# A two-group encoder block: the down products by Strassen's algorithm, right operands summed a phase earlier

## The chip, the cores and the metric

The kernel runs on one core of a Trainium2 chip. The metric is the time of one execution on the device, in microseconds (us). Before the change three runs gave a median of 2451.57 us (2447.15 to 2452.31).

## The reference

One layer is applied to two sequences with shared weights: 256 and 1024 tokens, each with 16 meta tokens in front. All is float32, the width is 1024, FF is 2816.

```
h = h + 0.5 * SwiGLU_1(RMSNorm(h))          # (silu(x Wg) * (x Wu)) Wd
u = RMSNorm(h) @ W_in                        # q, k, v of 4 heads; 512 channels for a pooling mixer
h = h + concat(diff_attention(q, k, v), pool(u)) @ W_out
h = h + 0.5 * SwiGLU_2(RMSNorm(h))
out = RMSNorm(h), meta tokens dropped
```

## The kernel before, in words

The 1296 tokens (1280 after the mixer, which drops one set of meta tokens; both sequences share the other) lie along the free axis, channels on the partitions: h is 8 chunks of 128 channels. Every float32 product is three matmuls (`mm3`, lines 161 to 163): both operands are split into a high and a low part, and high x high, low x high and high x low are added in one PSUM bank. The high part is a cast, on ScalarE (`hi_act`, line 146) or GpSimd (`hi_pool`, line 149); the low part is a subtraction, on VectorE (`lo_dve`, line 152) or GpSimd (`lo_pool`, line 155).

The gate and up products go by Strassen's algorithm (Winograd's form): tokens lie in four blocks of 324 (320), two blocks make a half, and the left operand is a pair of FF chunks. `s_parts` makes seven left operands out of the weights of a pair, four of them sums; seven right operands (`T_NAMES`: b11, t1, t2, b22, t3, b21, t4) lie split in SBUF for each half. `seven` runs the seven products in this order, adding in PSUM into three accumulators, A (b11, t2, t3, t4), C (t1, b22) and B (b21). ScalarE keeps three partial sums, VectorE adds the others, ScalarE takes silu of the gate, VectorE multiplies it with the up product (line 488), and SP stores the hidden tiles to device memory (line 490), four per pair of chunks and half. At the head of a feed-forward the first half runs alone for three pairs (`SINGLE1`, `SINGLE2`) while the right operands of the second half are made (`t_loaded`); then both halves run for eight pairs; then the second half runs alone for the first three.

The down product doesn't use the algorithm: for each pair of FF chunks `prep` loads hidden tiles of three blocks (272, 512 and 512 tokens; 256, 512, 512 in the second feed-forward) and splits them; for each of 8 output chunks and each block six matmuls fill a bank, and VectorE adds half of it to h (line 530). For the last pair it goes block by block, so that sums of squares and the norm of a finished block go on beside the next (`norm_tasks`, deferred through a list of small tasks that `pump` takes from between matmuls). The mixer's projections use the same three blocks: three projections first (`lead`), then the others; the value product takes tokens as left operands, in tiles of 128, 96 or 80 rows. At the kernel's end `finish` transposes h by token tiles, normalises and stores; the last block is two tiles.

All DMAs are issued on SP. Weights come through a ring of three raw buffers (`wraw`, 512 KB each) and five pairs of split ones (`wh`, `wl`). The order on each engine is set when the kernel is built: of the instructions whose inputs are expected to be ready, the one that stands first in the program. On the chip each engine then takes its queue in that order.

## Time and profile before

| | |
|---|---|
| median of three runs | 2451.57 us |
| the profiled execution | 2450.31 us, its span 2448.5 us |
| TensorE busy | 2336.4 us, 95% of the span |
| VectorE, ScalarE, GpSimd busy | 62%, 33%, 16% |
| TensorE's mean granted clock | 0.979 of full speed |
| DMA | 264.7 MB, 108 GB/s over the span |

Times are in microseconds from the span's start. PE is TensorE's matmuls, PEld its weight loads, DVE VectorE, ACT ScalarE, POOL GpSimd, SP the engine that issues DMAs. The first down stage runs from 612 to 933, the second from 2118 to 2437; the first gate and up phase from 54 to 612. Matmuls are pipelined, so the length shown for one is more than the distance to the next.

### The profile page before, as it was taken

The numbers are of one execution on the slowest core, as the hardware profiler recorded it, in microseconds if no ns is written. First come the engines' busy times: TensorE is split into PE (matmuls) and PEld (weight loads), VectorE is DVE, ScalarE is ACT, GpSimd is POOL, SyncE is SP. The second block draws the span as 40 slices with busy tenths as digits, with TensorE's granted clock in tenths as the row PEclk, the third lists the DMA queues.
The fourth block names the chain that finished last, engine by engine and source line by source line (L and its number), as shares of the span: only waits on it lengthen the run. The fifth ranks groups of instructions, "written<-read, shape, count | busy, mean of one in ns | idle before, by whom it ended". The sixth has DMA issues, their size and how long they took to land.

```text
span 2448.5 us, 38316 instructions
## 1 busy us (share of the span) xinstructions
PE 2336.4 (95%) x14578; PEld 2181.6 (89%) x14578; DVE 1506.1 (62%) x2834; ACT 803.8 (33%) x1705; POOL 387.6 (16%) x479
## 2 busy tenths in 40 slices
PE   5999999999999998999888898899999999999998
PEld 5899999999888887889778898889999999988886
DVE  7964545448676667344477747685455446667665
ACT  6533333335011123111377723453333334211113
POOL 0000000000111124111376743100000000021112
PEclk7999999999999999999999998999999999999999
DMA  8422222245232224545754154432122216323222
GB/s 234 118 80 72 65 64 75 70 150 174 77 96 79 82 71 134 167 145 159 186 134 124 49 166 154 133 96 74 57 80 73 74 57 222 116 82 96 86 69 86
DMA packets 294591, 264.67 MB, mean 108 GB/s; under 512 B 22048, under 2 KB 254072, under 8 KB 293896
## 3 DMA queue, kind: packets, MB, share of 16 engines
q1 hardware_dynamic: 294408, 262.24, 35.3%
q8 instruction: 114, 1.87, 0.3%
q14 instruction: 69, 0.57, 0.1%
HBM read 190.79 MB, written 75.61 MB: 109 GB/s over the span
## 4 chain that ended last, share of the span: by engine, by line
PE 82%; DVE 8%; DMA 4%; POOL 2%; issue 2%; ACT 1%; SPq 1%; POOLq 0%; ACTq 0%; DVEq 0%
PE bank L162 26%; PE bank L161 26%; PE bank L163 26%; DVE wl L152 1%; DMA v<-v_d 1%; PE bank L893 1%; PE pair L845 1%; PE pair L846 1%; PE bank L242 1%; DMA wraw<-in_ffn_w_up 1%; DMA wraw<-in_ffn_w_gate 1%; DMA cat<-cat_d 1%; POOL l L876 0%; POOL ry L223 0%; DVE h L328 0%
## 5 line engine op out<-in xcount | busy, mean ns | idle before, releaser
L152 DVE TENSOR_TENSOR wl<-wraw,wh 128x512 fp32r<-128x512 f32 x320 | 235.3, 740 | 296.1 <-ACT wh L146 219.8
L530 DVE SCALAR_TENSOR_TENSOR h<-bank,h 128x272 f32<-128x272 f32 (+2 forms) x528 | 313.1, 601 | 155.3 <-PE bank L163 151.3
L161 PE MATMUL bank<-hl,wh 128*128 128x512 f32 (+2 forms) x1056 | 380.4, 360 | 0.0
L162 PE MATMUL bank<-hl,wl 128*128 128x512 f32 (+2 forms) x1056 | 379.4, 359 | 0.0
L163 PE MATMUL bank<-hl,wh 128*128 128x512 f32 (+2 forms) x1056 | 379.1, 359 | 0.0
L146 ACT CAST hl<-hraw 128x272 fp32r<-128x272 f32 (+2 forms) x132 | 72.7, 552 | 517.2 <-PE bank L162 438.6
L155 POOL TENSOR_TENSOR hl<-hraw,hl 128x272 fp32r<-128x272 f32 (+1 forms) x44 | 34.7, 790 | 1239.9 <-ACT hl L146 1148.9
L163 PEld LDWEIGHTS bank<-hl,wh 128*128 128x128 f32 x1056 | 199.2, 189 | 31.6
L161 PEld LDWEIGHTS bank<-hl,wh 128*128 128x128 f32 x1056 | 199.2, 189 | 31.5
L162 PEld LDWEIGHTS bank<-hl,wl 128*128 128x128 f32 x1056 | 199.1, 189 | 31.4
L146 ACT CAST wh<-ws 128x512 fp32r<-128x512 f32 x224 | 138.4, 620 | 252.4 <-PE bank L163 156.0
L451 ACT COPY hid<-bank 128x324 f32<-128x324 f32 (+1 forms) x264 | 112.7, 427 | 279.5 <-PE bank L163 278.9
L152 DVE TENSOR_TENSOR wl<-ws,wh 128x512 fp32r<-128x512 f32 x224 | 153.7, 689 | 73.2 <-ACT wh L146 72.4
L149 POOL TENSOR_SCALAR wh<-wraw 128x512 fp32r<-128x512 f32 x152 | 115.1, 759 | 526.4 <-PE bank L163 245.2
L161 PE MATMUL bank<-t1h,wh 128*128 128x324 f32 (+1 forms) x352 | 110.3, 314 | 9.5 <-ACT wh L146 9.4
L162 PE MATMUL bank<-t1h,wl 128*128 128x324 f32 (+1 forms) x352 | 111.3, 316 | 4.0 <-DVE wl L152 3.9
L161 PE MATMUL bank<-t2h,wh 128*128 128x324 f32 (+1 forms) x352 | 110.2, 313 | 5.1 <-ACT hid L451 5.1
L162 PE MATMUL bank<-t4h,wl 128*128 128x324 f32 (+1 forms) x352 | 109.8, 312 | 3.1 <-DVE wl L152 3.0
L161 PE MATMUL bank<-t4h,wh 128*128 128x324 f32 (+1 forms) x352 | 109.4, 311 | 3.5 <-DVE hid L465 3.5
L161 PE MATMUL bank<-t3h,wh 128*128 128x324 f32 (+1 forms) x352 | 109.4, 311 | 1.8 <-ACT wh L146 1.8
L162 PE MATMUL bank<-t3h,wl 128*128 128x324 f32 (+1 forms) x352 | 109.7, 312 | 1.0 <-DVE wl L152 1.0
L161 PE MATMUL bank<-b21h,wh 128*128 128x324 f32 (+1 forms) x352 | 110.4, 314 | 0.3
(238 smaller groups left out, 6376.1 us busy)
## 6 DMA issues: line engine op xcount, KB each, us to landing
wraw<-in_ffn_w_gate SPq DMA_DIRECT2D x56, 512.0 KB
wraw<-in_ffn_w_up SPq DMA_DIRECT2D x56, 512.0 KB
hraw<-hid_d SPq DMA_DIRECT2D x88, 256.0 KB
wraw<-in_ffn_w_down SPq DMA_DIRECT2D x44, 512.0 KB
hid_d<-hid SPq DMA_DIRECT2D x88, 162.0 KB
hid_d<-hid SPq DMA_DIRECT2D x88, 160.0 KB
k<-k_d SPq DMA_DIRECT2D x32, 260.0 KB
h<-h_d SPq DMA_DIRECT2D x16, 512.0 KB
```

What stands on the lines that cost most here:

```text
L146: nc.scalar.copy(out=out, in_=in_)
L149: nc.gpsimd.tensor_scalar(out=out, in0=in_, scalar1=1.0, scalar2=1.0, op0=ALU.mult, op1=ALU.mult)
L152: nc.vector.tensor_sub(out, in_, hi.bitcast(F32))
L155: nc.gpsimd.tensor_sub(out, in_, hi.bitcast(F32))
L161: nc.tensor.matmul(out=ps, lhsT=wh, rhs=xh, start=first, stop=False, skip_group_check=on)
L162: nc.tensor.matmul(out=ps, lhsT=wl, rhs=xh, start=False, stop=False, skip_group_check=on)
L163: nc.tensor.matmul(out=ps, lhsT=wh, rhs=xl, start=False, stop=last, skip_group_check=on)
L242: nc.tensor.matmul(out=ps[:, j * m : (j + 1) * m], lhsT=r[:, j : j + 1].broadcast_to([m, P]), rhs=ident[:m, :m], start=True, stop=True,)
L451: nc.scalar.copy(out=to[s], in_=ps[s])
L530: nc.vector.scalar_tensor_tensor(out=h[b][:, m], in0=ps, scalar=0.5, in1=h[b][:, m], op0=ALU.mult, op1=ALU.add)
L845: nc.tensor.matmul(out=ps[:, m], lhsT=qs, rhs=kh[:, ks], start=True, stop=False)
L846: nc.tensor.matmul(out=ps[:, m], lhsT=qs, rhs=kl[:, ks], start=False, stop=True)
```

## The change

The hidden values no longer leave the gate and up phase as four tiles per pair and half but as the seven right operands of the down product: `up` forms t3, t1, t2 and t4 on VectorE by four subtractions and stores seven tiles. The down product runs by the same `seven`: the left operands are made by `s_parts` out of four quarters of the down weights (a pair of FF chunks by a pair of output chunks), and the inner sum runs over the pairs of a slice, `nk` of them. A slice is two pairs, the first one is one pair, so there are six slices for 11 pairs. Every product's PSUM sum is added to a quarter of h straight away (`ADDS`), 14 adds for each group of two output chunks (`mp`) and two halves, with no kept partial sums. Right operands lie in two pools of slots, x (ten) and y (32 in the first feed-forward, 26 in the second); those of the next slice are loaded through four staging tiles and split on ScalarE and VectorE while the present slice runs: `early` of them one after each product of the first groups, the rest in the last group, as slots come free. The last group of the last slice runs the halves one after the other, keeping the seven left operands. GpSimd makes no high parts in the down stage any more.

The halves of the first feed-forward are now blocks 0, 1 and 2, 3. The mixer uses the four blocks of 324: norms by block (one sum of squares instead of two), xm in the y slots, the first three projections advance together through the channels as xm's parts come (`pump` as needed), value tiles have 108 rows. At the end `finish` works by halves: five token tiles are left for after the last group.

```diff
-PAIRS1 = ((0, 2), (1, 3))
+PAIRS1 = ((0, 1), (2, 3))
...
+PRODUCTS = (("b11", "A", True), ("t1", "C", True), ("t2", "A", False), ("b22", "C", False), ("t3", "A", False), ("b21", "B", True), ("t4", "A", False))
...
+ADDS = dict(b11=(0, 0), t1=(1, 1), t2=(0, 1), b22=(0, 1), t3=(1, 1), b21=(0, 0), t4=(1, 0))
...
+            xh, xl = slot("y")
+            out.append((xh, xl))
...
+    def seven(parts, rhs, n, subs, after):
+        acc = {}
+        for name, a_, first in PRODUCTS:
+            wh, wl = next(parts)
+            k = wh.shape[1]
             for s in subs:
                 if first:
+                    acc[a_, s] = bank()[:, :n]
+                for c in range(k):
+                    mm3(acc[a_, s], (wh[:, c], wl[:, c]), rhs(s, name, c), first and c == 0, c == k - 1, not first)
                     pump()
             for s in subs:
+                after(name, s, acc[a_, s])
+    def gate_up(j, T, n, subs, wg, wu, hid, tp, bufs, raws=None):
...
+        def up(s, key, c, in_psum=False):
+            b = x[s, key] = g[s, key] if in_psum else c
+            nc.vector.tensor_mul(b, g[s, key], c)
+            if key != "b12":
+                out(s, key, b)
+            if key == "b22":
+                t3 = temp()
+                nc.vector.tensor_sub(t3, b, x[s, "b12"])
+                out(s, "t3", t3)
+            elif key == "b11":
+                t1 = x[s, "b12"]
+                nc.vector.tensor_sub(t1, t1, b)
+                out(s, "t1", t1)
+                t2 = x[s, "t2"] = temp()
+                nc.vector.tensor_sub(t2, x[s, "b22"], t1)
+                out(s, "t2", t2)
+            elif key == "b21":
+                t4 = temp()
+                nc.vector.tensor_sub(t4, b, x[s, "t2"])
+                out(s, "t4", t4)
...
+    IN_X = ("b11", "t1", "t2", "b22", "t3")
+    def down_tasks(h, places, n, hid, wd, pools_, y_bufs, st, single):
+        js = list(range(single, NF // 2)) + list(range(single))
+        slices = [js[:1]] + [js[i : i + 2] for i in range(1, len(js), 2)]
+        assert all(len(s) == 2 for s in slices[1:])
+        todo = deque()
+        T = [defaultdict(dict) for _ in slices]
+        box = {}
+        def slot(where):
+            return tuple(
+                pools_[where].tile([P, NS], F32R, tag=f"{where}{t}", name=f"{where}{t}", bufs=(y_bufs, 2 * len(IN_X))[where == "x"])[:, :n]
+                for t in "hl"
+            )
+        def load(i, name, s, jj):
+            raw = st.tile([P, NS], F32, tag="raw", name="raw", bufs=4)[:, :n]
+            nc.sync.dma_start(out=raw, in_=hid[slices[i][jj]][name][s])
+            return raw
+        def split(i, name, s, jj, where, raw):
+            th, tl = T[i][s, name][jj] = slot(where)
+            hi_act(th, raw)
+            lo_dve(tl, raw, th)
+        def lists(i):
+            two = len(slices[i]) - 1
+            ys = [(name, s, jj) for name in T_NAMES for jj in range(two + 1) for s in range(2) if jj < two or name not in IN_X]
+            xs = [(name, s, two) for name in IN_X for s in range(2)]
+            return [(i, *k, "y") for k in ys], [(i, *k, "x") for k in xs]
+        ahead = deque()
+        def plan(keys):
+            todo.extend(keys)
+        def fetch():
+            while todo and len(ahead) < 4:
+                key = todo.popleft()
+                ahead.append((key, load(*key[:4])))
+        def work(k=1):
+            for _ in range(k):
+                fetch()
+                if not ahead:
+                    return
+                key, raw = ahead.popleft()
+                split(*key, raw)
+            fetch()
+        def raw_w(i, mp):
+            raw = ring.tile([P, 4, 2 * P], F32, tag="wraw", name="wraw", bufs=3)
+            for jj, j in enumerate(slices[i]):
+                nc.sync.dma_start(
+                    out=raw[:, 2 * jj : 2 * jj + 2],
+                    in_=wd[2 * j * P : 2 * (j + 1) * P, 2 * mp * P : 2 * (mp + 1) * P].rearrange("(c p) n -> p c n", p=P),
+                )
+            return raw
+        def head_x():
+            ys, xs = lists(0)
+            plan(xs + ys)
+            work(len(xs))
+            box["raw"] = raw_w(0, 0)
+        def run_(done):
+            work(len(T_NAMES) * 2 - 2 * len(IN_X))
+            extra = pools_["y"]
+            early = y_bufs - 18
+            for i, sl in enumerate(slices):
+                nk = len(sl)
+                end = i + 1 == len(slices)
+                ys, xs = lists(i + 1) if not end else ([], [])
+                for mp in range(KC // 2):
+                    raw = box["raw"]
+                    nxt = (i, mp + 1) if mp + 1 < KC // 2 else (i + 1, 0)
+                    if nxt[0] < len(slices):
+                        box["raw"] = raw_w(*nxt)
+                    if mp == 0:
+                        plan(ys[:early])
+                        ys = deque(ys[early:])
+                        xs = deque(xs)
+                    v = raw.rearrange("p (j k) n -> p j k n", k=2)[:, :nk]
+                    quads = [v[:, :, k, f * P : (f + 1) * P] for f in range(2) for k in range(2)]
+                    def rhs(s, name, c):
+                        return T[i][s, name][c]
+                    def after(name, s, ps):
+                        fi, ti = ADDS[name]
+                        hs = h[:, 2 * mp + fi, places[s][ti] : places[s][ti] + n]
+                        nc.vector.scalar_tensor_tensor(out=hs, in0=ps, scalar=0.5, in1=hs, op0=ALU.mult, op1=ALU.add)
+                        if end:
+                            if name == "t4":
+                                done(s, mp)
+                        elif s:
+                            if mp < KC // 2 - 1:
+                                work(1)
+                            else:
+                                work(4)
+                                plan(q.popleft() for q in (ys, xs, ys, xs) if q)
+                                fetch()
+                    if end and mp == KC // 2 - 1:
+                        kept = []
+                        def keep():
+                            for p in s_parts(*quads, st, extra):
+                                kept.append(p)
+                                yield p
+                        seven(keep(), rhs, n, (0,), after)
+                        seven(iter(kept), rhs, n, (1,), after)
+                    else:
+                        seven(s_parts(*quads, st), rhs, n, (0, 1), after)
+                        if mp == KC // 2 - 1:
+                            assert not ys and not xs
+                            work(len(todo) + len(ahead))
+        return head_x, run_, slot
...
+        for b in range(len(BS1)):
+            pss = [bank()[:, :NS] for _ in lead]
+            for c in range(KC):
+                while len(xm[b]) <= c:
+                    pump()
+                for w, ps in zip(ws, pss):
+                    mm3(ps, w[c], xm[b][c], c == 0, c == KC - 1)
+            for i, ps, (r, out) in zip(lead, pss, res):
+                out(i, r, b, ps)
...
+            for b, (s, n) in enumerate(BS1):
+                m = n // 3
...
+        def half_in(t, half):
+            p = bank()
+            for c in range(4):
+                cc = 4 * half + c
+                nc.tensor.transpose(out=p[:, c * P : (c + 1) * P], in_=h[:, cc, t * P : (t + 1) * P], identity=ident)
+            o = y[t, half] = y_tile()
+            nc.scalar.activation(out=o, in_=p, func=AF.Square, accum_out=ss[:, 2 * t + half : 2 * t + half + 1])
+            if half == 0:
+                nc.vector.tensor_mul(o, p, g_fin[:, :512])
             else:
+                nc.vector.tensor_mul(o, p, g_fin[:, 512:])
+        def rstd(ts):
+            k = len(ts)
+            tot = small.tile([P, 8], F32, tag="ftot", name="ftot", bufs=2)[:, :k]
+            v = ss[:, 2 * ts[0] : 2 * ts[0] + 2 * k].rearrange("p (t f) -> p t f", f=2)
+            nc.vector.tensor_add(tot, v[:, :, 0], v[:, :, 1])
+            r = rstd_cols(tot, P, k, 1.0 / D)
+            for i, t in enumerate(ts):
+                ps[t] = r[:, i : i + 1]
+        def write(t, half):
+            k0 = t * P
+            dst = a["y_prompt"][0][k0 : k0 + P] if k0 < 256 else a["y_sample"][0][k0 - 256 : k0 - 256 + P]
+            o = y[t, half]
+            if half:
+                nc.vector.tensor_scalar(out=o, in0=o, scalar1=ps[t], scalar2=None, op0=ALU.mult)
+            else:
+                nc.scalar.mul(out=o, in_=o, mul=ps[t])
+            nc.sync.dma_start(out=dst[:, 512 * half : 512 * half + 512], in_=o)
+        def finish(s, mp):
+            ts = list(range(NT // 2 * s, NT // 2 * (s + 1)))
+            if mp == 1 and s == 1:
+                tasks.extend(spread("y", [lambda t=t: half_in(t, 0) for t in range(NT // 2)], 1))
+            elif mp == KC // 2 - 1:
+                fs = [lambda t=t: half_in(t, 1) for t in ts]
+                fs += [lambda: rstd(ts)]
+                fs += [lambda t=t, k=k: write(t, k) for t in ts for k in (1, 0)]
+                if s == 0:
+                    fs += [lambda t=t: half_in(t, 0) for t in range(NT // 2, NT)]
+                tasks.extend(("y", f) for f in fs)
+        down(finish)
```

## Rows read from the trace of the kernel before

**Rows 1.** Page, part 1: busy time of each engine

```profile
PE 2336.4 (95%) x14578; PEld 2181.6 (89%) x14578; DVE 1506.1 (62%) x2834; ACT 803.8 (33%) x1705; POOL 387.6 (16%) x479
```

**Rows 2.** Windows: us; PE, PEld, DVE, ACT, POOL busy (x), clock, DMA share, GB/s

```profile
640.50:668.80 28.30, 28.30 (x145) 24.00 (x144) 19.54 (x33) 3.33 (x6) 4.69 (x7) 1.00 0.29 83
...
922.00:930.00 8.00, 5.39 (x24) 4.33 (x24) 5.21 (x12) 3.83 (x8) 3.99 (x6) 0.80 0.41 152
```

**Rows 3.** Windows, both token halves in the first gate and up

```profile
118.00:534.00 416.00, 415.69 (x2797) 415.30 (x2798) 208.19 (x358) 138.40 (x285) 0.00 (x0) 1.00 0.24 73
```

**Rows 4.** Windows, one half alone: three of the six from 66 to 114

```profile
66.00:74.00 8.00, 7.44 (x47) 6.87 (x47) 7.87 (x18) 4.54 (x11) 0.00 (x0) 1.00 0.36 97
...
74.00:82.00 8.00, 6.31 (x39) 5.55 (x39) 7.82 (x17) 3.30 (x8) 0.00 (x0) 1.00 0.66 201
...
106.00:114.00 8.00, 7.41 (x47) 6.67 (x46) 7.82 (x16) 3.77 (x8) 0.00 (x0) 1.00 0.39 128
```

**Rows 5.** Timeline of PE, first matmuls of two products: start, length, engine, line, operation

```profile
401.80 0.31 PE L161 MATMUL bank<-b21h,wh 128*128 128x324 f32 x1
...
405.36 0.31 PE L161 MATMUL bank<-t4h,wh 128*128 128x324 f32 x1
```

**Rows 6.** Timeline of PE, last pair of the first down stage

```profile
894.41 0.40 PE L161 MATMUL bank<-hl,wh 128*128 128x512 f32 x1
...
895.10 0.40 PE L161 MATMUL bank<-hl,wh 128*128 128x512 f32 x1
...
896.50 0.29 PE L161 MATMUL bank<-hl,wh 128*128 128x272 f32 x1
...
902.50 0.39 PE L161 MATMUL bank<-hl,wh 128*128 128x512 f32 x1
```

**Rows 7.** Timeline of PE, two value tiles, and a window of that stage

```profile
1034.35 0.28 PE L161 MATMUL bank<-wh,xh 128*96 128x256 f32 x1
...
1039.98 0.28 PE L161 MATMUL bank<-wh,xh 128*80 128x256 f32 x1
...
1040.00:1060.00 20.00, 20.00 (x172) 20.00 (x171) 5.15 (x9) 3.73 (x8) 0.00 (x0) 1.00 0.29 92
```

**Rows 8.** Timeline of DVE where its queue is dense

```profile
70.74 0.50 DVE L461 TENSOR_TENSOR hid<-bank,hid 128x324 f32<-128x324 f32 x1
71.15 0.69 DVE L152 TENSOR_TENSOR wl<-wraw,wh 128x512 fp32r<-128x512 f32 x1
...
898.34 1.12 DVE L530 SCALAR_TENSOR_TENSOR h<-bank,h 128x272 f32<-128x272 f32 x3
```

**Rows 9.** Groups by line and shape: count | busy, mean ns | idle before

```profile
L530 DVE SCALAR_TENSOR_TENSOR h<-bank,h 128x512 f32<-128x512 f32 x352 | 240.6, 687 | 148.8 <-PE bank L163 148.5
...
L530 DVE SCALAR_TENSOR_TENSOR h<-bank,h 128x272 f32<-128x272 f32 x88 | 38.3, 437 | 3.2 <-PE bank L163 0.2
...
L461 DVE TENSOR_TENSOR hid<-bank,hid 128x324 f32<-128x324 f32 x44 | 21.8, 495 | 17.6 <-PE bank L163 15.5
```

**Rows 10.** Timeline, stores of one product; chain of waits, one load of 160 KB

```profile
612.62 0.94 SPq L490 DMA_DIRECT2D hid_d<-hid  x2
...
1439.41 2.86 DMA cat<-cat_d
```

**Rows 11.** Timeline of PE, sums and rows of the mixer's norm [idle before <-releaser]

```profile
905.29 1.09 PE L297 MATMUL bank<-ones,acc 128*68 128x1 f32 x16
...
909.11 1.01 PE L242 MATMUL bank<-ident,rr 68*128 68x68 f32 x8
...
925.34 1.82 PE L297 MATMUL bank<-ones,acc 128*128 128x1 f32 x14 [2.61 <-DVE acc L265]
...
936.59 1.62 PE L242 MATMUL bank<-ident,rr 128*128 128x128 f32 x8 [2.33 <-DVE rr L229]
```

**Rows 12.** Timeline, the last down matmul and the last stores

```profile
2436.02 0.28 PE L163 MATMUL bank<-hl,wh 128*128 128x256 f32 x1
...
2442.84 2.83 SPq L1337 DMA_DIRECT2D out_y_prompt<-y  x4
```

More of the change, by code (lines that the diff above doesn't have):

```diff
@@ L429, in s_parts @@
         yield h3, l3
-        yield parts_of(a12, hi_act)
-        yield parts_of(a22, hi_act)
-    def seven(w, j, T, n, subs, tp, temp, sink, raws=None):
-        parts = s_parts(w, j, tp, raws)
-        A, B, C, s1, s2, s5 = {}, {}, {}, {}, {}, {}
-        def product(acc, k, first):
-            part = next(parts)
+        yield plain(a12)
+        yield plain(a22)
+    def seven(parts, rhs, n, subs, after):
[3 more added lines that the diff above has]
+            k = wh.shape[1]
@@ L440, in product @@
             for s in subs:
                 if first:
-                    acc[s] = bank()[:, :n]
-                th, tl = T[s][k]
-                for c in range(4):
-                    mm3(acc[s], (part[0][:, c], part[1][:, c]), (th[:, c], tl[:, c]), first and c == 0, c == 3, not first)
+                    acc[a_, s] = bank()[:, :n]
+                for c in range(k):
+                    mm3(acc[a_, s], (wh[:, c], wl[:, c]), rhs(s, name, c), first and c == 0, c == k - 1, not first)
                     pump()
-        def keep(to, ps):
```

344 lines of the change are left out of this document (125 added, 219 removed).

## The prediction

> **What bounds the kernel now.** I read the page first: TensorE is busy 95% of the span, VectorE 62%, DMA little [rows 1]. So I asked, stage by stage, what TensorE and VectorE do (the windows). In a pair of FF chunks of the down stage TensorE is busy the whole 28.3 us and VectorE 19.5 us; at the stage's end TensorE stalls and its granted clock falls to 0.80 [rows 2]. The middle of gate and up looks alike (TensorE 415.7 of 416 us, VectorE 208) [rows 3]; but while one half of the tokens runs alone at the head of a feed-forward, VectorE is busy 7.8 to 8.0 of every 8 us over six rows and TensorE is not full [rows 4]. The chain of waits is mostly matmuls and tells little here; pitches do (start to start of one kind, from the timeline), since durations overlap.
>
> TensorE's pitches. In one product of gate and up 24 matmuls of 324 columns take 3.56 us, 148.5 ns each [rows 5]. In the down stage 512 columns take 233 ns (894.41 to 895.10 is three) and 272 take 125 (48 in 6.00 us) [rows 6]; 256 in the value product take 117.5 (48 in 5.63) [rows 7]. That is 0.46 ns a column whatever the width (320: 146.7): cutting wide matmuls into more, narrower ones costs nothing here, leaving out columns pays in full.
>
> VectorE's pitches. An operation of 324 that reads PSUM starts 0.41 us before the next (70.74 to 71.15), though it lasts 0.50; three adds of 272 take 1.12 us, and with 0.437 for the last [rows 9] that is 0.342 each [rows 8]. About 1.04 ns a column (687 less 437 ns over 240 columns [rows 9]) and 0.06 to 0.07 us more. I take 0.405 for 324, 0.40 for 320, and by the same line 0.33 for 256 and 0.20 for 128, which have no dense row here (above nothing and below 0.342).
>
> **The change part by part.**
>
> Down, TensorE. Before, a pair is 48 times (125.2 + 2 x 233.3 ns) = 28.4 us in the first feed-forward, 48 x (117.5 + 466.6) = 28.0 in the second; eleven pairs 312.7 and 308.4. After, a pair is 4 x 7 x 2 x 3 = 168 matmuls: 24.95 and 24.65 us, eleven 274.4 and 271.1. **Gain 75.6 us**, if TensorE stays the bound.
>
> Down, VectorE. A slice of two pairs has 4 groups of 256 output rows, and in each 14 adds from PSUM into h (0.405) and 11 operations on weights of 256 columns (7 low parts, 4 sums; 0.33); and 28 low parts of right operands for the next slice. That is 56 x 0.405 + 44 x 0.33 + 28 x 0.405 = 48.5 us, against 49.9 of TensorE. Per pair VectorE goes from some 17 us of pitch (19.5 busy) to 24.2, and TensorE from 28.4 to 24.95: two engines of equal length. GpSimd, which made high parts of weights, has nothing left here, and ScalarE takes them.
>
> The slice of one pair, the first, is the clear loss. It has as many adds and splits for half the products: 22.7 + 44 x 0.20 + 11.3 = 42.8 us of VectorE against 24.95 of TensorE. At the 98% that VectorE reaches in [rows 4] it lasts 43.7, with the fill some 44: 19 us over TensorE in each feed-forward, **38 in all**. If VectorE never waits it is 36; if it reached only the 86% that TensorE does beside it in [rows 4] (278 matmuls in the six rows, 133 in the three shown, x 148.5 ns, in 48 us) it is 50. TensorE would work some 60% of that time in short bursts. A stretch with 6.31 of 8 us busy in short bursts has clock 1.00 [rows 4]; one with 5.39 of 8 and a stall of 2.6 us in it 0.80 [rows 2, 11]; at the lower of the two levels the slice would take 50 us, 12 more in all. I take no fall.
>
> The four full slices of two pairs that prepare another (eight in all). The splits are not spread evenly. In the first feed-forward 14 fall in the first two groups of a slice and 14 in the last, whose VectorE work is 9.3 + 5.7 = 15.0 us against 12.5; in the second, with 26 slots instead of 32, 8 and 20: 17.3 against 12.3. VectorE may lag about one product (1.78 us) before the next product on the same bank waits for its add; the third group, without splits, takes the lag back. That leaves 0.7 us a slice in the first and, part of the splits sliding into the next slice, 2.5 in the second: 13. For two engines both over 97% full I add 1 us each, 8. **21 in all**; the ends are 0 (perfectly even) and 51 (VectorE at 86%: 56 us a slice).
>
> The last slice has no splits, but its last group runs the halves one after the other, so a bank's next product starts 1.0 us after the last matmul of the one before, of which that matmul's length (0.31) and the add (0.50) leave 0.2 (lengths in [rows 5, 9]); behind a waiting matmul all of TensorE's queue stands. Four times, two halves, two stages, 0.25 us each. **4**; ends 0 and 10.
>
> DMAs. Per half and pair 7 stores instead of 4 on SP, and 154 loads of right operands and 44 of weights instead of 66 and 22 per stage. At 0.47 us an issue (two in 0.94 [rows 10]) that is 93 us of SP in 300, and DMA's share was 0.29 [rows 2]: no cost. A load of this size lands in 2.9 us [rows 10]; with 4 staging tiles that gives a split each 0.8 us, just the rate of the last group. The four extra subtractions per pair and half wait in VectorE before weight work. Where both halves run VectorE has half its time free [rows 3]: nothing. While one half runs at the head, VectorE is full [rows 4]: 2 x 3 x 4 x 0.405 = 9.7 us, of which I take **7** (0 to 10). The buffers of products turn 10 a pair instead of 7 through 9; each is free a product or more before its turn.
>
> Mixer by 324. Value tiles go from 11 to 12: 2 x 24 more matmuls of 256 columns, 5.6 us on TensorE, which never waits there [rows 7]; the other projections 594 ns against 592: 0.6. **6.** The change of blocks at the end of the first down stage has its stalls now (2.6 and 2.3 us, and the clock [rows 2, 11]); after, the first half's norm has 6 us of matmuls above it, less than the chain of sums, row and split, and four blocks queue for it. I take no change, between 6 less and 20 more.
>
> The end. Before, two token tiles are left after the last matmul: 12.2 us from 2436.3 to the end of the span. After, five: three more squares and products (0.6 each, by the line above), and ten stores instead of four behind each other on SP, where four take 2.8 with their waits [rows 12]. **6** more; 0 to 12.
>
> Sum: -75.6 + 38 + 21 + 4 + 7 + 6 + 6 = +6.4, on the profiled execution's 2450.3 (span 2448.5 and 1.8 around it), which lies 1.3 below the median: 2456.7 there, **2458 us** as a median, 0.26% slower.
>
> Adds from PSUM come 0.342 us apart at 272 columns, 0.06 over the columns' time [rows 8]. A rule of the Trainium skill speaks against that pitch: Perfetto Trace Analysis, section Optimizing Scalar/DVE Operations, gives a VectorE operation an overhead of about 60 ns on SBUF and about 125 ns on PSUM. The trace disagrees with its second figure; by it an add of 324 would take an estimated 0.46 us and the change end near 2481.
>
> **Rivals.**
> *VectorE fits under TensorE* (not slower). Place: the eight full slices. For it: 48.5 is less than 49.9, and the splits have a slice's length to be done in. Against it: 15 and 17 us of work in groups of 12.5. Then 21 becomes 3, bank waits 1, head 3, end 3: 2456.7 - 18 - 3 - 4 - 3 = 2429, as a median 2430.
> *VectorE sets the pace in all slices*, because its queue is in order and an add waiting for TensorE holds weight parts that TensorE needs. For it: no stage of the trace runs both engines full. It decides where VectorE works less than some 90% of a slice; at the 86% above +30 in the full slices, +12 in the first and +4 of bank waits: 2504.
> *Adds that don't overlap the operation behind them.* Each then costs its duration, 0.495 us [rows 9]: 0.09 x 56 = 5 us a slice, 10 in the two first; the eight full ones have 53.5 of VectorE against 49.9, 3.5 each, 28, of which 8 is the 1 us each already in: 2488. The dense rows speak against it.
> *Norm rows in series.* Each mixer block's row is made only when its turn comes, behind the block before it: three times the way from sums to row, 3.8 us with VectorE free and 11.3 with it shared (905.3 to 909.1, 925.3 to 936.6 [rows 11]), 7 in the middle: +20, 2478. Against it: sums can be slipped in wherever TensorE waits.
>
> **How the numbers follow.** Forecast 0.37 (its own range 2447 to 2470), fits 0.34, VectorE's pace 0.16, norm rows 0.09, adds without overlap 0.04. Less than 0.2% (5 us) either way can't be told from no change. Faster: nearly all of the second case and a little of the first, 0.36; same: a third of the first and some of the second, 0.17; slower 0.47. The range is cut inside the outer cases on both sides: 2424 to 2486.
>
> **What would show it.** After: some 3,700 down matmuls of 324 and 320 columns at 0.147 to 0.149 us pitch; a first slice of 44 us with VectorE full and TensorE at 60%; full slices of 51 and 53 us, with TensorE's waits on VectorE in their last group; low parts and adds at 0.405 us. TensorE full in the full slices would prove the first rival; slices of 54 or more the second; idle TensorE of 7 us before each mixer block the fourth. The forecast is wrong if the first slice takes under 38 us, or if narrow matmuls don't keep their pitch.

## The result and the profile after

The changed kernel takes 2532.93 us (four runs, 2531.91 to 2534.04), the kernel before, beside it, 2450.23: ratio 1.0339, interval 1.0321 to 1.0357. That is 75 us above the forecast of 2458 and outside its range. The same kernel at another time gave 2522.98 (2519.83 to 2526.77; ratio 1.0306, 1.0288 to 1.0323), so a difference of some 10 us between two sessions is no finding by itself; below, single stages are compared, with both profiles of the changed kernel beside them.

Stages, from the first and last matmul or addition of each in the traces (us):

| stretch | before | after | change | forecast | after, second profile |
|---|---|---|---|---|---|
| start, to the first gate and up matmul | 34.7 | 35.8 | +1.1 | 0 | 34.8 |
| gate and up, first / second | 577.8 / 568.4 | 591.2 / 577.2 | +22.2 | +7 | 590.6 / 577.4 |
| down, first / second, to the last addition | 324.6 / 318.6 | 326.7 / 333.3 | +16.8 | -12.6 | 324.6 / 329.5 |
| mixer, to the first attention step | 224.2 | 250.7 | +26.5 | +6 | 249.7 |
| attention, output projection | 388.8 | 394.9 | +6.1 | 0 | 391.3 |
| end | 11.4 | 20.0 | +8.6 | +6 | 20.0 |
| span | 2448.5 | 2529.8 | +81.3 | +6.4 | 2518.1 |

The page's first part (busy us, share, instructions) answers to [rows 1]: TensorE works less, 92% now, and VectorE more.

```profile
PE 2325.6 (92%) x15434; PEld 2264.9 (90%) x15434; DVE 1753.6 (69%) x3850; ACT 985.5 (39%) x2247; POOL 274.8 (11%) x342
```

The windows (columns as in [rows 2]) show the first slice of the first down stage, then one full slice cut into its four groups of outputs, and a full slice of the second stage.

```profile
627.00:677.20 50.20, 35.82 (x183) 31.66 (x181) 46.51 (x130) 21.23 (x60) 0.00 (x0) 0.86 0.51 151
...
731.80:747.10 15.30, 12.81 (x83) 12.00 (x82) 13.44 (x35) 6.04 (x17) 0.00 (x0) 1.00 0.54 153
747.10:760.00 12.90, 12.72 (x85) 12.31 (x84) 12.57 (x33) 4.12 (x11) 0.00 (x0) 1.00 0.44 120
760.00:772.30 12.30, 12.30 (x85) 12.30 (x84) 11.96 (x31) 3.46 (x10) 0.00 (x0) 1.00 0.14 44
772.30:785.90 13.60, 13.40 (x90) 13.09 (x89) 13.31 (x34) 8.45 (x21) 0.00 (x0) 1.00 0.65 177
...
2281.20:2339.20 58.00, 52.64 (x338) 50.94 (x336) 51.70 (x130) 22.15 (x56) 0.00 (x0) 0.97 0.39 117
```

In the third group, which has no splits, TensorE is never idle: 12.30 us of 12.30, and half of the 24.95 forecast for a pair is 12.47 (VectorE's 11.96 are durations that overlap). The loss stands at the slice's edges: in the first group VectorE is busy 13.44 of 15.30 us and TensorE 12.81, so both stand still at times; the fourth group, with half of the splits, takes 13.60. The first slice is VectorE's (46.51 of 50.20). First slices take 50.1 and 49.4 us, full ones 54.1 to 55.8 and 55.3 to 57.9, last ones 57.2 and 59.0 (second profile: first slices 48.0 and 48.1).

TensorE's waits over the whole run (total us, times, longest) name two that were smaller before, `wl` and `wh`; the first two lines are the kernel before, the others the changed one:

```profile
PE bank L162 <- DVE wl L152: 15.3, 19, 6.1
...
PE bank L161 <- ACT wh L146: 11.2, 9, 3.8
...
PE bank L162 <- DVE wl L152: 52.0, 53, 6.1
PE bank L161 <- ACT wh L146: 34.7, 24, 5.2
PE bank L161 <- DMA v<-v_d: 25.9, 4, 8.3
PE bank L161 <- DVE h L616: 15.9, 21, 1.9
```

One of the second kind, at the edge of a slice, in two timelines (start, length, operation, idle time before and what ended it), first ScalarE's:

```profile
734.08 0.46 ACT L146 CAST yh<-raw 128x324 fp32r<-128x324 f32 x1 [2.59 <-DMA raw<-hid_d8t]
734.44 0.40 ACT L146 CAST wh<-ws 128x256 fp32r<-128x256 f32 x1
```

then TensorE's:

```profile
731.95 0.31 PE L161 MATMUL bank<-xh,wh 128*128 128x324 f32 x1
732.09 0.31 PE L162 MATMUL bank<-xh,wl 128*128 128x324 f32 x1
732.25 0.31 PE L163 MATMUL bank<-xl,wh 128*128 128x324 f32 x1
734.89 0.57 PE L161 MATMUL bank<-yh,wh 128*128 128x324 f32 x2 [2.34 <-ACT wh L146]
```

ScalarE stood 2.59 us before the cast of a right operand whose load had not landed, an operand of the next slice that nobody needed yet. The cast of the current weights was queued behind it, and TensorE waited 2.34 us for that. The same rows show the pitch of 324 columns: 0.14 to 0.16 us, as [rows 5].

### The profile page after: what moved, and what is told of

Same layout as the page of the kernel before. It is cut to its first block, busy times and chain, and to the rows that moved or that the text cites. A ratio compares the mean times of both kernels' runs of the same rounds, so it can differ in the third digit from the quotient of the medians.

```text
span 2529.8 us, 42335 instructions
## 1 busy us (share of the span) xinstructions
PE 2325.6 (92%) x15434; PEld 2264.9 (90%) x15434; DVE 1753.6 (69%) x3850; ACT 985.5 (39%) x2247; POOL 274.8 (11%) x342
## 4 chain that ended last, share of the span: by engine, by line
PE 69%; DVE 14%; DMA 9%; ACT 3%; issue 3%; POOL 2%; SPq 1%; ACTq 0%; POOLq 0%; DVEq 0%
PE bank L162 22%; PE bank L161 22%; PE bank L163 21%; DVE h L616 3%; DVE wl L152 3%; DMA v<-v_d 2%; ACT wh L146 1%; DVE yl L152 1%; PE pair L957 1%; DMA wraw<-in_ffn_w_up 1%; PE bank L1005 1%; PE pair L958 1%; PE bank L242 1%; DVE xl L152 1%; DMA wraw<-in_ffn_w_gate 1%
## 5 line engine op out<-in xcount | busy, mean ns | idle before, releaser
L152 DVE TENSOR_TENSOR wl<-wraw,wh 128x512 fp32r<-128x512 f32 (+2 forms) x374 | 220.8, 600 | 271.7 <-ACT wh L146 216.6
L146 ACT CAST wh<-ws 128x512 fp32r<-128x512 f32 (+2 forms) x414 | 211.7, 513 | 448.9 <-PE bank L163 256.5
L162 PE MATMUL bank<-yh,wl 128*128 128x324 f32 (+1 forms) x1128 | 358.1, 318 | 16.5 <-DVE wl L152 16.4
L161 PE MATMUL bank<-yh,wh 128*128 128x324 f32 (+1 forms) x1128 | 341.6, 321 | 25.8 <-DVE h L616 12.0
L163 PE MATMUL bank<-yl,wh 128*128 128x324 f32 (+1 forms) x1128 | 353.4, 315 | 0.0
L616 DVE SCALAR_TENSOR_TENSOR h<-bank,h 128x324 f32<-128x324 f32 (+1 forms) x672 | 321.4, 489 | 30.8 <-PE bank L163 24.2
L152 DVE TENSOR_TENSOR wl<-ws,wh 128x512 fp32r<-128x512 f32 (+2 forms) x414 | 229.5, 557 | 79.0 <-ACT wh L146 77.2
L161 PEld LDWEIGHTS bank<-yh,wh 128*128 128x128 f32 x1128 | 211.5, 193 | 40.5 <-ACT wh L146 15.0
L162 PEld LDWEIGHTS bank<-yh,wl 128*128 128x128 f32 x1128 | 217.0, 192 | 23.8 <-DVE wl L152 21.8
L163 PEld LDWEIGHTS bank<-yl,wh 128*128 128x128 f32 x1128 | 216.4, 192 | 0.6 <-POOL yl L155 0.5
```

The costliest lines, as they stand in the source:

```text
L146: nc.scalar.copy(out=out, in_=in_)
L152: nc.vector.tensor_sub(out, in_, hi.bitcast(F32))
L161: nc.tensor.matmul(out=ps, lhsT=wh, rhs=xh, start=first, stop=False, skip_group_check=on)
L162: nc.tensor.matmul(out=ps, lhsT=wl, rhs=xh, start=False, stop=False, skip_group_check=on)
L163: nc.tensor.matmul(out=ps, lhsT=wh, rhs=xl, start=False, stop=last, skip_group_check=on)
L616: nc.vector.scalar_tensor_tensor(out=hs, in0=ps, scalar=0.5, in1=hs, op0=ALU.mult, op1=ALU.add)
```

## Experiments

Each ran beside the kernel before; ratios are to it.

**VectorE's low parts moved to GpSimd**

```
 def split(i, name, s, jj, where, raw):
-            lo_dve(tl, raw, th)
+            lo_pool(tl, raw, th)
```

> The changed kernel with one edit: in the down stages the low parts of the right operands (28 a full slice, 14 for the first) are made by GpSimd, which is idle there, not by VectorE. Theory A (VectorE sets the pace of the slices: 48.5 us of operations at dense pitch, in an order that also waits for TensorE, against 49.9 of TensorE): VectorE keeps 37.2 us in a full slice and 31 in the first, so full slices fall from 54.1 to 55.9 us and 55.3 to 58.0 us to 50 or 51, the first ones from 50 to about 36, the last ones (no splits in them) stay at 57 and 59; together some 70 us less, about 2463. Theory B (the slices are long because banks, weights and adds wait for one another in turn, whatever VectorE's load): full slices stay above 53, total above 2510. Theory C (GpSimd, at 0.945 us for such an operation, needs 13.2 us for the 14 of a slice's last group and delivers the operands late): VectorE falls below 75% busy and yet slices stay above 53, with TensorE waiting for GpSimd.

Measured: 2525.71 us (1.0309, 1.0292 to 1.0327), between the two times of the unchanged kernel: no gain in all. The down stages took 323.8 and 321.3 us, the second one 8 to 12 less, but the second gate and up phase took 583.2, 6 more. First slices 46.0 and 45.8, full ones 53.4 to 58.4: theory B's numbers, but none of the three theories had the reason. Groups of VectorE in the first slice (count | busy us, mean ns of one | idle before), changed kernel:

```profile
L616 DVE SCALAR_TENSOR_TENSOR h<-bank,h 128x324 f32<-128x324 f32 x56 | 25.0, 489 | 2.5 <-PE bank L163 2.0
...
L152 DVE TENSOR_TENSOR wl<-ws,wh 128x128 fp32r<-128x128 f32 x13 | 3.6, 284 | 0.0
```

and with the low parts on GpSimd:

```profile
L616 DVE SCALAR_TENSOR_TENSOR h<-bank,h 128x324 f32<-128x324 f32 x57 | 24.2, 485 | 0.3
L152 DVE TENSOR_TENSOR wl<-ws,wh 128x128 fp32r<-128x128 f32 x13 | 8.7, 703 | 0.7 <-ACT wh L146 0.7
...
L155 POOL TENSOR_TENSOR yl<-raw,yh 128x324 fp32r<-128x324 f32 x22 | 19.6, 911 | 64.2 <-ACT yh L146 61.0 <-PE bank L163 2.8
```

An operation with two inputs in SBUF lasts 703 ns instead of 284 beside GpSimd's of 911; the additions that read PSUM stay at 485. The Trainium skill (GPSIMD Engine Reference, section Specifications) states that the two engines' SBUF interfaces are shared, and that VectorE instructions with two SBUF inputs contend with GpSimd. These rows agree. VectorE is as full as before (44.76 us of the 46.0 of that slice), so the run says nothing on how much of the loss is VectorE's load.

**No sums, no stores of them, in gate and up**

```
             if key != "b12":
                 out(s, key, b)
-            if key == "b22":
-                t3 = temp()
...
+            else:
+                out(s, "t1", b)
...
```

> The changed kernel, leaving out the four subtractions that form right operands in the gate and up phase, and three of the seven stores; the down stages load other stored tiles in place of the sums, so the down products are not the reference's. The loads, splits and products of the down stages are as many as in the changed kernel. Gate and up took 591.2 and 577.3 us against 577.6 and 568.5 before. Theory A (the subtractions and their stores cost all of that): 578 and 569 again, total 22 less, about 2511. Theory B (the loss has to do with the new tiling of the buffers and the order of the work, not with these operations): 588 or more and 575 or more.

Measured: 2506.31 (1.0233, 1.0218 to 1.0248). Gate and up 582.4 and 572.1, against 591.2 and 577.2 (second profile 590.6 and 577.4): some 14 of the 22 us come from the sums and their stores, less than theory A had and more than B. The head of the first (pairs 2, 3 and the first with both halves) is back at 30.3, 27.7 and 49.9 us, just as before the change. The first pair after the two halves part is not: 31.4 us, 30.8 in the changed kernel, 28.4 before.

**Stores kept, subtractions left out**

```
-                t3 = temp()
-                nc.vector.tensor_sub(t3, b, x[s, "b12"])
-                out(s, "t3", t3)
+                out(s, "t3", b)
...
```

> The changed kernel, leaving out only the four subtractions; all seven stores per half and pair stay (the tiles at hand are stored under the names of the sums, so the down products are not the reference's). Theory A (it is VectorE's time for the subtractions): gate and up fall to some 580 and 570, as in the run without both. Theory B (it is the stores: they are still on their way when the next scope takes over the buffers, and VectorE's first weight sum there waited 2.06 us for one): the heads of both stages gain some 5 and 1 us, but the step from both halves to the second half alone stays at 30.8 and 32.4 us for the first single pair, against 28.4 and 28.1 before.

Measured: 2511.64 (1.0256, 1.0241 to 1.0271). Gate and up 586.0 and 574.1: the subtractions cost 5.2 and 3.1, the stores 3.6 and 2.0. Neither theory alone. The step from both halves to one took 33.4 us here in the first feed-forward, so it doesn't hang on the sums alone. VectorE's timeline there, in the changed kernel, first weight sum of the new scope:

```profile
546.61 0.69 DVE L417 TENSOR_TENSOR ws<-wraw 128x512 f32<-128x512 f32 x1 [2.06 <-DMA hid_d10b<-hid]
```

and in the run without sums, where the first sum ran at once, the second:

```profile
539.30 0.69 DVE L420 TENSOR_TENSOR ws<-ws,wraw 128x512 f32<-128x512 f32 x1 [4.16 <-DMA hid_d10b<-hid]
```

These sums neither read nor write a hidden tile, so the new scope must lie where the last products' buffers were, and VectorE waits until their stores have left. With four stores it waits too; in the kernel before, the same two sums waited for no store. In the second feed-forward that pair takes 32.4 us in the changed kernel, 28.1 before, 28.3 and 29.5 in these two runs: there the sums do bear on it. What sets its length is left open.

**Deferred tasks in the mixer's lead**

```
                     mm3(ps, w[c], xm[b][c], c == 0, c == KC - 1)
+                    pump()
```

> The changed kernel with one edit: in the first three projections of the mixer one deferred task is taken after each group of three matmuls (as the kernel before did), instead of only when the next block's chunk is missing. Theory A (the norm rows of the four blocks are made one after the other, each only when its turn has come): TensorE's waits of 9.6 us between 940 and 1000 fall to 4 or less, the clock stays up, and the way from the last down product to the first attention step falls from 280.6 to about 266; total about 2518. Theory B (the waits stem from the last slice's end, where the second half's sums are late whatever the order behind them): 276 or more, total 2528 or more.

Measured: 2517.29 (1.0276, 1.0257 to 1.0294); mixer 246.9 against 250.7 and 249.7. TensorE's waits from the last addition to the first attention step, changed kernel:

```profile
PE bank L242 <- DVE rr L229: 4.4, 2, 2.2
PE bank L850 <- DMA onehot<-in_onehot: 3.7, 1, 3.7
PE bank L161 <- ACT yh L146: 2.8, 3, 1.1
```

and with the tasks spread:

```profile
PE bank L850 <- DMA onehot<-in_onehot: 3.6, 1, 3.6
PE bank L242 <- DVE rr L229: 1.6, 1, 1.6
PE bank L161 <- ACT yh L146: 1.3, 2, 1.1
PE bank L163 <- POOL yl L155: 0.5, 1, 0.5
```

The waits for rows and operands fall from 7.2 to 3.4 us, the stage by 3 to 4 and not by the 14 announced (the total is theory A's 2518, within the spread between two runs): rows in series are a small part. The windows of the changed kernel show another:

```profile
953.70:961.70 8.00, 8.00 (x44) 7.99 (x43) 6.22 (x13) 2.71 (x6) 5.12 (x6) 0.68 0.88 307
...
977.70:989.70 12.00, 9.21 (x46) 9.00 (x46) 6.69 (x16) 3.70 (x8) 4.06 (x5) 0.72 0.00 0
989.70:1005.00 15.30, 11.91 (x67) 11.28 (x65) 5.88 (x15) 3.67 (x8) 3.52 (x5) 0.78 0.00 1
```

TensorE works in bits of a block, and the granted clock goes down to its lower level for part of each window: busy time times what is missing to 1.00, an estimate of what that costs, is 2.6 + 2.6 + 2.6 us, and 1.6 more from 1005 to 1035 (0.94). In the kernel before it is 1.7 us (one window of 8 us at 0.79).

**Prefetch a group later**

```
-                    if mp == 0:
+                    if mp == 1:
                         plan(ys[:early])
```

> The changed kernel with one edit: the 14 (second feed-forward: 8) right operands that a full slice loads and splits ahead for the next one are taken in its second and third group of outputs instead of its first and second. The first group of a slice now lasts 15.2 to 15.6 us (second feed-forward 16.1 to 17.8), the third, without splits, 12.3. Theory A (VectorE's and ScalarE's queues are overfull in the first group, which has the rest of the last group's splits and the prefetch): first groups fall to about 13 and 14 us, full slices from 54.1 to 55.9 us and 55.3 to 58.0 to 51 or 52 and 53 or 54, total some 23 less, about 2510. Theory B (it is the last group's operands, late for the first products of the next slice, whatever stands behind them): full slices stay at 54 and 55 or more, total above 2525.

Measured: 2517.55 (1.028, 1.026 to 1.03), 5 us under the nearer time of the unchanged kernel. Full slices 50.6 to 54.8 and 53.2 to 55.9. First groups fall (two to 12.3 and 12.0), but the fourth group in front of each of them rises to 17.3 and 17.7. Inconclusive: part of the loss only moves.

**First slice plain**

```
+                    if i == 0:
+                        plain(mp, v[:, 0], after0)
...
+                        for k in range(2):
+                            mm3(ps, (wh[:, k, cs], wl[:, k, cs]), T[0][s, f"b{k + 1}{ti + 1}"][0], k == 0, k == 1)
+                        hs = h[:, 2 * mp + fi, places[s][ti] : places[s][ti] + n]
+                        nc.vector.scalar_tensor_tensor(out=hs, in0=ps, scalar=0.5, in1=hs, op0=ALU.mult, op1=ALU.add)
```

> The changed kernel with one edit: the first slice of each down stage, the one with a single pair of FF chunks, is computed without Strassen's algorithm, as the kernel before did (192 matmuls of 324 or 320 columns instead of 168, 32 additions into h instead of 56, 4 low parts of weights of 512 columns instead of 44 operations of 128, 8 right operands instead of 14). TensorE then needs 28.5 us and VectorE 32 x 0.405 + 4 x 0.6 + 28 x 0.405 = 26.7, where it needed 42.8. Theory A (these slices take 50.1 and 49.4 us since VectorE is full): 29 to 31 us each, total some 40 less, about 2493. Theory B (they take so long since loads and splits for the next slice come at the pace of four staging tiles, 28 of them): 40 us or more each, total above 2513.

Measured: 2488.86 (1.0167, 1.0148 to 1.0185). First slices 33.3 and 34.1 us instead of 50.1 and 49.4 (48.0 and 48.1). The window of the first, and of the full slice behind it:

```profile
626.60:659.80 33.20, 32.10 (x216) 31.84 (x215) 29.44 (x73) 14.13 (x33) 0.00 (x0) 1.00 0.70 203
659.80:710.90 51.10, 49.32 (x321) 47.85 (x322) 49.88 (x125) 21.93 (x55) 0.00 (x0) 1.00 0.46 131
```

With a seventh more columns TensorE is done some 15 us earlier, since VectorE has 32 additions and 4 weight operations instead of 56 and 44. That is theory A, if 3 us over its 29 to 31; the loads of the 28 operands go along with it in 33 us, so B falls. The edit also takes 18 operands, not 14 and 8, before the slice's last group; what that did by itself was not tried.

**Six staging tiles in the first feed-forward**

```
+        depth = 6 if y_bufs == 32 else 4
-            raw = st.tile([P, NS], F32, tag="raw", name="raw", bufs=4)[:, :n]
+            raw = st.tile([P, NS], F32, tag="raw", name="raw", bufs=depth)[:, :n]
...
+                                if mp == KC // 2 - 2 and name == "t4" and depth > 4:
+                                    plan(q.popleft() for q in (ys, xs)[: depth - 4] if q)
+                                    fetch()
```

> The changed kernel with one edit, in the first feed-forward's down stage only: six staging tiles for loaded right operands instead of four, and two loads planned a product earlier. Theory A (the order and amount of VectorE's work set the slices): full slices stay at 54 to 56 us in both stages, total within 5 us of 2533. Theory B (ScalarE stands before loads that have not landed, and the casts of weights behind it; at 734 us it waited 2.59 us for one, and TensorE 2.34 for the weight's cast): in the first stage full slices fall by 2 to 3 us each, in the second they stay; total some 10 less.

Measured: 2511.49 (1.0256, 1.0235 to 1.0277). The edit also plans two loads a product earlier. Full slices of the first stage 52.4 to 53.1, mean 52.8, against 54.8 and (second profile) 54.9; those of the second stage, where nothing was changed, mean 56.3 against 56.2 and 56.0. Theory B. TensorE's waits in the four slices with six tiles:

```profile
PE bank L161 <- ACT wh L146: 3.3, 6, 0.7
PE bank L162 <- DVE wl L152: 2.4, 4, 0.6
```

and with four, in the second profile of the changed kernel:

```profile
PE bank L161 <- ACT wh L146: 6.7, 3, 2.4
PE bank L162 <- DVE wl L152: 3.9, 9, 2.1
```

**The edits together**: first slice plain, prefetch a group later, six staging tiles, tasks in the lead, and the look-up

```
-            tasks.extend([("bias", None)] * 3 + [("bias", lambda i=i: look_up(i))])
+            tasks.extend([("bias", None)] * (3 if i else 5) + [("bias", lambda i=i: look_up(i))])
```

> The changed kernel with the edits of the last three runs and the deferred tasks in the mixer's lead together, and the first look-up of the bias table two tasks later (TensorE waited 3.7 us there for its load). If the parts add up as their theories say (40 for the plain first slices, 23 for the later prefetch, 8 for the staging, 10 for the lead, 4 for the look-up) the total is some 85 below 2533, about 2448, level with the kernel before. If VectorE's pace in the last group of each slice keeps the full slices at 53 or more, 2465.

Measured: 2465.7 (1.0068, 1.0047 to 1.0088). Down stages 295.9 and 305.3 us: 42 less than before the change. Gate and up (594.0, 578.6), mixer (242.2) and end (20.3) keep the whole slower. The total is the second one announced, but its condition, 53 us or more, holds for three of the eight full slices alone (51.9 to 52.6 and 50.3 to 55.4).

**Strassen in the down stage for the middle pairs only**

```
-        slices = [js[:1]] + [js[i : i + 2] for i in range(1, len(js), 2)]
+        slices = [[0]] + [[j, j + 1] for j in range(single, NF // 2, 2)] + [[j] for j in range(1, single)]
...
+            if j < PLAIN:      # PLAIN = 3: store the four hidden tiles, form no sums
+                return
...
+                            for b in range(4):      # last pair: block by block
+                                for m, w in enumerate(whole):
+                                    plain(i, m, w, b // 2, b % 2, lambda: None)
+                                    done(b, m)
```

> Strassen's algorithm in the down products only for the eight pairs of FF chunks that the gate and up phase computes for both halves at once, where VectorE has half its time free; the three pairs that it computes half by half are plain products in the down stage (one first, two last, the last one block of tokens by block), so their subtractions and the three stores of sums are gone. With it the edits of the combination: six staging tiles (in both stages), prefetch a group later, deferred tasks in the mixer's lead, later first look-up. Theory A (VectorE is the scarce engine at the head of gate and up and in the slices of one pair, and nowhere else do the sums cost): gate and up fall from 594 and 579 us to about 582 and 572, as in the run without sums and stores; the down stages from 296 and 305 to 290 to 300, a plain pair costing 28.5 us against 25 and its stalls; the mixer and the end some 5 us each; total 2435 to 2445, below the kernel before (2450). Theory B (the loss in gate and up is in the change of scopes, and the full slices stay at 52 to 55 us whatever is beside them): 2455 or more.

Measured: 2457.78 (1.0039, 1.0025 to 1.0052). Gate and up 582.8 and 573.6, mixer 229.9, end 12.4: as much as theory A has, or more; full slices 48.6 to 54.8. The total is theory B's, for a reason that neither had. The last plain slice of the first feed-forward took 57.9 us, where that of the second took 37.1 and the other plain ones 28.1 to 32.4. TensorE's waits in it:

```profile
PE bank L291 <- DVE acc L261: 11.2, 2, 8.2
PE bank L162 <- DVE h L610: 1.5, 1, 1.5
```

**Sums given time**

```
-    ... gains["norm_mix"], slot, temp1, xm[b], (2, 4)
+    ... gains["norm_mix"], slot, temp1, xm[b], (10, 8)
-            return tp.tile([P, NB], F32, tag="y", name="y", bufs=12)
+            return tp.tile([P, NB], F32, tag="y", name="y", bufs=8)
-        ... pools_, 26, hp, SINGLE2)
+        ... pools_, 29, hp, SINGLE2)
```

> The kernel of the last run with three edits: ten and eight tasks instead of two and four stand between a block's last addition, its sums of squares and its row in the mixer's norm; the second feed-forward's output tiles turn in 8 buffers instead of 12; and with the room its down stage has 29 slots for right operands instead of 26, so 11 instead of 8 are taken ahead of a slice's last group. In the last run the last plain slice of the first feed-forward took 57.9 us where the other plain ones took 28.1 to 30.4; TensorE waited 11.2 us there for sums of squares (8.2 at once), and its granted clock was 0.50 for about 10 us. Theory A (the matmul of the sums stands in TensorE's queue too early, and the clock falls behind the wait): that slice falls to 30 to 36 us and the total by 20 to 28, to 2430 to 2438, below the kernel before (2449). Theory B (the chain of squares, sums and rows is as long as the slice whatever its place): 50 us or more, total 2450 or more.

Measured: 2431.7 us, ratio 0.9929, 0.9916 to 0.9943: 0.7% below the kernel before, clear of the noise. The last slice of the first feed-forward falls from 57.9 to 37.1 us, a little over theory A's 30 to 36, and its clock rises from 0.80 to 0.96; the total is theory A's. The window of that slice in the run before this one:

```profile
882.10:939.90 57.80, 42.15 (x245) 39.72 (x244) 39.06 (x92) 21.05 (x46) 22.33 (x26) 0.80 0.18 64
```

and in this one, with the last slice of the second feed-forward:

```profile
882.80:919.90 37.10, 34.51 (x231) 33.59 (x230) 29.32 (x71) 17.43 (x38) 17.63 (x22) 0.96 0.19 71
2380.50:2417.60 37.10, 36.01 (x261) 35.05 (x260) 28.82 (x73) 15.04 (x40) 2.25 (x3) 1.00 0.23 88
```

Its stages: gate and up 583.2 and 573.8, down 301.6 and 303.4, mixer 232.8, end 12.4. Against the combination two runs before, gate and up are 16 us shorter, the mixer 9, the end 8; the down stages are 4 longer. In the second down stage, where there are now 29 slots, full slices take 51.5 us on average instead of 52.7.

**The changed kernel once more**

> The changed kernel as it is, once more, to see how far its time and its stages vary from call to call: the runs with one edit were each compared with the kernel before on their own chip, and gains of 7 to 20 us were read against the 2533 of another call. Theory A (the stages repeat to 2 or 3 us): 2525 to 2535, each full slice within 1.5 us of the first profile. Theory B (a tenth of the differences read so far is chance): the total differs by 10 us or more.

Measured: 2522.98 us, as told above. Theory B: the total moved by about 10 us, single full slices by up to 2.0 us (their mean in a stage by 0.2 at most), first slices by up to 2.2, gate and up by less than 1. So the first, fourth and fifth experiments (2525.7, 2517.3, 2517.6) show no effect on the total that this spread leaves standing, and are read by waits, groups and durations alone. The third and the seventh (2511.6, 2511.5) lie 11 us under the nearer time of the unchanged kernel, hardly more than the spread, and rest on their stages.

## Why the prediction failed

The side was right (slower, 0.47), the size was not; with stages missed by 15 to 29 us, the side of a forecast of +6 was little more than luck. By its steps:

**Down, TensorE, -75.6: right.** 324 columns still take 0.149 us, 320 take 0.147; groups without splits take 12.2 to 12.3 us, half a pair. The forecast would have been wrong if narrow matmuls lost their pitch; they didn't.

**VectorE's durations: right.** In a stretch where its queue is dense an addition from PSUM and a split follow each other every 0.40 us:

```profile
778.26 0.49 DVE L616 SCALAR_TENSOR_TENSOR h<-bank,h 128x324 f32<-128x324 f32 x1
778.66 0.49 DVE L152 TENSOR_TENSOR xl<-raw,xh 128x324 fp32r<-128x324 f32 x1
779.07 0.49 DVE L616 SCALAR_TENSOR_TENSOR h<-bank,h 128x324 f32<-128x324 f32 x1
...
761.89 0.42 DVE L434 TENSOR_TENSOR ws<-wraw 128x256 f32<-128x256 f32 x1
762.22 0.49 DVE L616 SCALAR_TENSOR_TENSOR h<-bank,h 128x324 f32<-128x324 f32 x1
```

An operation of 256 columns starts 0.33 us before the next, as estimated. So the rival of adds that don't overlap falls: reading PSUM (0.40 us) costs here what reading SBUF (0.41 us) costs. The larger overhead on PSUM that the Trainium skill gives (Perfetto Trace Analysis, section Optimizing Scalar/DVE Operations) is not borne out by these rows.

**First slices, 38: too small by 11.5** (8 by the second profile). The mechanism was right (VectorE 93% of the slice, TensorE 71%; taking VectorE's work away gave some 15 us each). The measured 50.1 and 49.4 are the upper end: by pitch, VectorE's 42.8 us are 85% of 50.1, near the 86% named there, where the forecast took 98%. "I take no fall" of the clock was wrong too: after a wait of 6.0 us (the longest for `wl`) it was 0.50 to 0.54, the lower level, for 10 us of the first one. TensorE's waits for `wl` in that slice, and three windows of it:

```profile
PE bank L162 <- DVE wl L152: 12.2, 7, 6.0
...
637.00:642.00 5.00, 0.00 (x0) 0.00 (x0) 4.50 (x11) 2.08 (x6) 0.00 (x0) 0.94 0.66 193
642.00:647.00 5.00, 4.41 (x16) 4.28 (x16) 4.65 (x14) 2.81 (x8) 0.00 (x0) 0.50 0.61 166
647.00:652.00 5.00, 3.81 (x16) 3.54 (x15) 3.70 (x12) 1.99 (x7) 0.00 (x0) 0.54 0.50 145
```

**The eight full slices, 21: the step that failed most, by 26.** They took 444.2 us where TensorE's columns need 396.8, so 47 instead of 21. The step weighed VectorE's work against TensorE's group by group and let the third group take the lag back. It did, but most of the loss is in the first group, 15.1 us on average in the first stage and 16.6 in the second, where both engines wait, and most of the rest in the fourth, 14.0 and 15.1. A cause that was left out is ScalarE: it casts right operands and weights in one queue, and the step "DMAs ... no cost" counted SP's time and the splits' rate and not who stands behind a split whose load is late. In the first stage, two more staging tiles with two loads planned earlier took 2 of the 5 us a slice. The second stage had no such run. There TensorE's waits over the four full slices name VectorE more than ScalarE:

```profile
PE bank L162 <- DVE wl L152: 7.8, 8, 1.5
PE bank L161 <- DVE h L616: 5.2, 6, 1.3
PE bank L161 <- ACT wh L146: 3.6, 4, 1.7
```

And the forecast's own numbers warned there: its 0.8 us a split is "just the rate of the last group" for 14 splits in 12.5 us, but with 20 in 12.3 a split has 0.6. Of the rest, experiment five moved part without removing it; how much is VectorE's uneven work was not isolated, and stays open.

**Last slices, 4.** They took 57.2 and 59.0 us, 17 over TensorE's columns. But the down stages before took 22 over theirs (643.2 against 621.1), which the forecast, taking columns from columns, left out: against them the ends gained 5 where 4 were to be lost. 11.5 and 26 less 9 is what the down stage missed, 29.

**Gate and up, 7: 22 measured.** "Where both halves run ... nothing" is exact: 349.3 us for the last seven of those pairs in both kernels. The head cost 12.4 (8.5 and 3.9); in the first feed-forward a third of that was the stores, which the forecast had at nothing. Unforeseen are the last three pairs, where one half runs alone again: 4.9 more in each stage. Without sums and stores 4.5 and 2.2 of that stay. "Each is free a product or more before its turn" looked at the turn within a scope, not at the next scope's tiles on the same memory; how much of the 9.8 is that wait was not isolated.

**Mixer, 6 + 0: 26.5.** Value tiles and pitches are 6.2 as counted, not measured apart. The transition was taken at nothing, with 20 more as its bound, and the bound came: some 10 us of TensorE's idle time more (12.1 against 2.1: rows, operands, the look-up's load) and, by the estimate above, 8 of clock. The rival "norm rows in series" had the size but not the cause, as its experiment shows. Finishing the last pair block by block brought the stage to 232.8; among the edits of that run this one was not isolated.

**End, 6: 8.6.** Attention's 6.1 was 2.5 in the second profile, and no term.

So the rival "VectorE sets the pace in all slices" was near on the slices (it had 56 us a full slice and 50 the first, and its sign, 54 or more, came), though its cause was not isolated, and the misses in the other stages came on top. The error behind the range: rivals in different stages were given chances as if one excluded the other. Their prices add: 2458 + 46 for the down stage + 20 in the mixer would have been 2524, near what was measured, though partly by luck: 46 is more than the 29 that the down stage missed, and the 15 in gate and up no rival had.

## What to carry to other kernels

An algorithm that saves an eighth of the matmul columns pays only where the other engines have room for its additions: here the pairs whose sums fall into a half-idle VectorE gain; for the single ones, between the eighth run and the tenth, the down stages gave up 4 us (9 without what the 29 slots gave back) where gate and up, without their sums and stores, won 16; other edits lie between these runs too. Using it for eight pairs of eleven, with the smaller edits above, is 0.7% faster where using it for all was 3.4% slower. For each engine ask not only how much work it has but what stands in its queue behind an instruction that waits for a load. And price rivals by stage, then add those that can come together.

## What the runs showed of the hardware

GpSimd is no free helper for VectorE: beside its operations of 0.91 us, VectorE's with two SBUF inputs went from 284 to 703 ns, while those with one input in PSUM kept 485 to 489.
